# Seven-product blocks in four parts, token factors first, and three weight halves split inside the passages of a two-layer trunk

## The chip, the cores and the metric

The kernel runs on one core of a Trainium2 chip. Its engines work side by side and in the order of their own queues: TensorE (PE) multiplies matrices, and the loading of its stationary operand has a row of its own (PEld); VectorE (DVE) and ScalarE (ACT) work on elements; GpSimd (POOL) and SyncE (SP) issue transfers here. The metric is the device time of one execution in microseconds (us), as the median of several runs. Before the change it is 2310.19 us (three runs, 2307.84 to 2311.49).

## The reference, cut to what matters

256 tokens of width 2048 pass through two layers. Each layer is a mixer (HGRN2 in layer 0, gated linear attention, GLA, in layer 1) and a squared-ReLU MLP of width 8192, each with a norm ahead of it, a norm behind it and a residual add. All is float32.

```python
def rmsnorm(x, w):
    y = xf * lax.rsqrt(jnp.mean(xf * xf, axis=-1, keepdims=True) + NORM_EPS)
    return (y * w.astype(jnp.float32)).astype(x.dtype)

def sqrelu_mlp(h, w_up, w_down):
    u = jax.nn.relu(h @ w_up)
    return (u * u) @ w_down

    for i in range(DEPTH):
        hn = rmsnorm(h, norm_mix_pre[i])
        ...
        h = h + rmsnorm(m, norm_mix_post[i])
        f = sqrelu_mlp(rmsnorm(h, norm_mlp_pre[i]), mlp_w_up[i], mlp_w_down[i])
        h = h + rmsnorm(f, norm_mlp_post[i])
```

## The kernel before, in words

**Two parts per number.** Each float32 matrix operand is split into a rounded part `hi`, made by ACT (L103), and a remainder `lo`, made by DVE (L107); a product is three matmuls (hi·hi, hi·lo, lo·hi) that accumulate. Weights come as chunks of 1 MB in three buffers (`raw`); a chunk is two halves of 128x1024, and each half is split into one of five buffers for `hi` and one of five for `lo` (pool `wsp`). The activations are kept transposed and split (`xhl`).

**Column products.** `gemmT` (L146, L149) makes 128 columns of a result, transposed, from one chunk: 16 matmuls of 512 columns with the `hi` weights, and 16 of 256 with the `lo` weights. `fold` (L155, L156) adds the two parts up. The factor per token (the reciprocal of the norm's root) isn't multiplied into the activations; it is applied to the results: `rrow` (L301, L303) spreads the factors `rs` of the 256 tokens over a tile `rr`, and each folded column product of an MLP is multiplied by it in L537. After it come the square and its split (L539 to L541).

**MLP.** The 8192 features are eight groups `g` of 1024. `up(g)` makes a group's features in eight column products, four for group 0, whose first half comes out of the passage. `combine` (L507 to L512) makes from four of these, by pairs, the sums of activations `as` (`sums_of_a`); they live in memory that the next group's sums reuse. The product of a group with two of the four column blocks of `w_dn` is a 2x2 block product, made with seven block products in place of eight: `seven(g)`. Of the seven, three use plain weights, four use sums of blocks of `w_dn`. These sums (tiles `run` and `Q`, `bs` in the rows) are made by transfers: `begin_run` and `begin_q` load a block on SP's queue (L563, L572), and `add_to` adds another block to it on POOL's queue (L558). Each block product is 12 matmuls of 512 columns into a bank of PSUM, `sa`, `sb` or `sc`, and two weight halves to split; `put` (L578, L580) then adds the bank to the result. The next product into the same bank waits for that. The other two column blocks of `w_dn` are done plainly (`plain`, 48 matmuls and four halves each).

**Order.** A planner orders the instructions on each engine: it takes them in the order of the program's text where they are ready by its own model of time, and pulls later ones ahead where earlier ones aren't. For group 0 and 1 the text is: `up(0)`; the first column product of `up(1)`; all of `seven(0)`; the other seven column products of `up(1)`. From there `down(g)` places the four parts of `seven(g+1)` between the chunks of `plain(g, 2)` and `plain(g, 3)`; `seven` is a generator that yields between its parts.

**Passages.** `transition` is the passage from one sub-layer to the next, three in all: HGRN to MLP 0, MLP 0 to GLA, GLA to MLP 1. It ends the last output block, norms, adds the residual (L340, one instruction per quarter row `n` and token half `t`), transposes `h` on PE (`T_in`, L182), scales and splits it (`T_out`, ACT L193 and DVE L195), and runs the first block of the next sub-layer on weights split ahead (`ahead`, eight halves): `nxt(0, j)` for the tokens of half 0, `nxt(1, j)` for half 1. Inside `manual_schedule` the instructions of PE, ACT, DVE and POOL keep the order of the text; the planner may still put instructions from outside the block between them. The squares of `h` for the token factors (L283, eight of them, `token_rstd`) end the block, and the loop over `nxt(1, j)` stands outside it.

Of the kernel before, what the change touches and what calls it, by code (L numbers as in the profile page):

```python
# [30 lines left out]
def trunk(  # L31
# [77 lines left out]
    def split(raw, into=None):  # L109
# [2 lines left out]
        split_lo(raw, half)  # L112
        return half

    def split_chunk(wap, idx):

        raw = load_chunk(wap, idx)
        return [split(raw[:, hf, :]) for hf in range(2)]

    def mm_half(ps, half, hf, xs, t, nk, kks=(0, 1), cs=slice(0, NB)):  # L120

# [88 lines left out]
    def start(which, w, base):  # L210

        X = Xhl(KT)
        xs = big.tile([P, KT, T], F32, tag="big", name="xs")
        ps = [psmm.tile([P, NB], F32, tag="mm", name=nm("mm")) for _ in range(NT)]
        early = []
        part = small.tile([P, NT, 4], F32, tag="tp", name=nm("tp"))

        def input_quarters(t, qs):  # L220
            for q in qs:
                c = slice(q * NB, (q + 1) * NB)
                nc.sync.dma_start(h[:, t, c], x[t * P:(t + 1) * P, c])
            for q in qs:
                square(part, t, q)

        def next_chunk(c):
            raw = wraw.tile([P, 2, 1024], F32, tag="raw", name=nm("raw"))
            for j in range(2):
                nc.sync.dma_start(raw[:, j, :], w[c].rearrange("p (k n) -> p k n", k=2)[:, j, :])  # L230
            ahead[c] = w, raw
            early.append(gemmT(w, c, X, *((psmm, "mm") if c < 2 else (pssc, "sc"))))

        with tc.manual_schedule(engines=ALL | {mybir.EngineType.SP}):
            for hf in range(KT // 2):
                if hf % 2 == 0:
                    raw = wraw.tile([P, 2, 1024], F32, tag="raw", name=nm("raw"))
                    src = w[base + hf // 2].rearrange("p (k n) -> p k n", k=2)
                for n in range(2 if hf == 0 else 1):

                    m = 2 if hf else 1
                    ks = slice(2 * hf + n, 2 * hf + n + m)
                    cs = slice(n * NB, (n + m) * NB)
                    first = hf == 0 and n == 0
                    nc.sync.dma_start(xs[:, ks, :], xT[:, ks, :])
                    (nc.scalar if first else nc.sync).dma_start(raw[:, hf % 2, cs], src[:, hf % 2, cs])
                    if first:
                        nc.sync.dma_start(prew, npre)
                        A.activation(warm, epsb, AF.Sqrt)
                        for _ in range(4):  # L250
                            idle = pstr.tile([P, T], F32, tag="tr", name=nm("idle"))
                            PE.matmul(idle, bc(epsb, [P, P]), bc(epsb, [P, T]), start=True, stop=True)
                    for k in range(2 * hf + n, 2 * hf + n + m):
                        hi, lo = X.both(k)[:, 0, :], X.both(k)[:, 1, :]
                        g = prew[:, which, k:k + 1]
                        A.activation(hi, xs[:, k, :], AF.Copy, scale=g)
                        V.scalar_tensor_tensor(lo, xs[:, k, :], g, hi.bitcast(F32),
                                               ALU.mult, ALU.subtract)
                    if n == 0:
                        half = (wsp.tile([P, 1024], F32R, tag="hi", name=nm("hi")),  # L260
                                wsp.tile([P, 1024], F32R, tag="lo", name=nm("lo")))
                    A.activation(half[0][:, cs], raw[:, hf % 2, cs], AF.Copy)  # L262
                    V.tensor_tensor(half[1][:, cs], raw[:, hf % 2, cs],  # L263
                                    half[0][:, cs].bitcast(F32), ALU.subtract)
                    if hf == 0:
                        for t in range(NT):
                            mm_half(ps[t], half, hf, X, t, KT, (n,))
                if hf:
                    for t in range(NT):
                        mm_half(ps[t], half, hf, X, t, KT)  # L270
            next_chunk(0)
            next_chunk(1)
            input_quarters(0, (0, 1))
            next_chunk(2)
            input_quarters(0, (2, 3))
            nc.sync.dma_start(ident, ident_in)
            next_chunk(3)
            input_quarters(1, range(4))
            rs = rstd_sum(part)
        return X, rs, ps, early  # L280

    def square(part, t, q):
        A.activation(tok(), h[:, t, q * NB:(q + 1) * NB], AF.Square, accum_out=part[:, t, q:q + 1])  # L283

    def token_rstd():
        part = small.tile([P, NT, 4], F32, tag="tp", name=nm("tp"))
        for t in range(NT):
            for q in range(4):
                square(part, t, q)
        return rstd_sum(part)  # L290

    def rstd_sum(part):
        ss = col(NT)
# [48 lines left out]
    class Next:  # L342

        def __init__(self, w, base, big_first=False):
            self.w, self.base, self.raws, self.parts = w, base, [], []
            self.room = self.rooms(big_first)

        def rooms(self, big_first):  # L350
# [39 lines left out]
    def transition(w, base, nk, xs, post, add, which, ahead):  # L390
# [41 lines left out]
        with tc.manual_schedule(engines=ALL):  # L432
            for j in range(4):
                last(0, j)
            first_use(0)
            last(1, 0)
            last(1, 1)
            post.rstd(0)
            ahead.hi()
            post.residual(0, 0)  # L440
            last(1, 2, (0,))
            T_in(0, 0)
            post.residual(1, 0)
            post.residual(2, 0)
            T_out(0, 0)
            last(1, 2, (1,))
            last(1, 3)
            post.residual(3, 0)
            T_in(0, 1)
            T_out(0, 1)  # L450
            nxt(0, 0)
            first_use(1)
            T_in(0, 2)
            nxt(0, 1)
            post.rstd(1)
            T_out(0, 2)
            post.residual(0, 1)
            T_in(0, 3)
            nxt(0, 2)
            T_out(0, 3)  # L460
            nxt(0, 3)
            ahead.lo()
            post.residual(1, 1)
            nxt(0, 4)
            ahead.split()
            T_in(1, 0)
            T_out(1, 0)
            nxt(0, 5)
            post.residual(2, 1)
            T_in(1, 1)  # L470
            nxt(0, 6)
            T_out(1, 1)
            post.residual(3, 1)
            T_in(1, 2)
            nxt(0, 7)
            T_out(1, 2)
            T_in(1, 3)
            T_out(1, 3)
            rs = token_rstd()
        for j in range(KT // 2):  # L480
            nxt(1, j)
        return X, rs, psn


    def mlp(layer, w_up, w_dn, X, rs, ps0, then=None):
# [27 lines left out]

        sa = {}

        def up(g):

            U = Xhl(GK)
            uT[g] = U
            a = {}  # L520
            js = [j + h for j in range(HK) for h in (0, HK)]
            if g == 0:
                for t in range(NT):
                    s = tok()
                    A.activation(s, ps0[t], AF.Relu, scale=rs[t])
                    A.activation(s, s, AF.Square)
                    ps = transpose4(lambda j: s[:, j * P:(j + 1) * P])
                    put_split(ps, U, 0, t)
                    raw = tok().rearrange("p (a n) -> p a n", a=4)
                    A.copy(raw, ps)  # L530
                    for j in range(HK):
                        a[j, t] = raw[:, j, :]
                rr.append(rrow(rs))
                js = range(HK, GK)
            for j in js:
                u = fold(gemmT(w_up, g * GK + j, X))
                V.scalar_tensor_tensor(u, u, 0.0, rr[0], ALU.max, ALU.mult)  # L537
                hi, lo = U.both(j)[:, 0, :], U.both(j)[:, 1, :]
                A.activation(hi, u, AF.Square)  # L539
                A.activation(u, u, AF.Square)  # L540
                V.tensor_tensor(lo, u, hi.bitcast(F32), ALU.subtract)  # L541
                for t in range(NT):
                    a[j, t] = u[:, t * P:(t + 1) * P]
                if j == js[0]:
                    yield
                    sa[g] = sums_of_a(g)
                if j >= HK:
                    i = j - HK
                    combine(sa[g][i], a[i, 0], a[j, 0], a[i, 1], a[j, 1])

        def block(g, h, n):
# [106 lines left out]
                pass  # L658

        for g in range(NG):  # L660
            it = up(g)
            next(it)
            if g == 0:
                begin_run(0)
                begin_q(0)
            if g == 1:
                rest(seven(0))
            rest(it)
            if g:
                down(g - 1)  # L670
# [349 lines left out]
        post = Post(1)  # L1020
        return outproj(w_gout, O, post, then)

    st = hgrn((2, w_up0, 0))
    st = mlp(0, w_up0, w_dn0, *st, then=(1, w_gin, 16))
    st = gla(*st, then=(3, w_up1, 0))
    mlp(1, w_up1, w_dn1, *st)


# [70 lines left out]
```

## Time and profile before

| | us |
|---|---|
| median of three runs | 2310.19 |
| the profiled execution | 2309.34 |
| its span, first to last instruction | 2307.6 |
| PE busy in the span | 2274.4 (99%) |
| DVE busy | 1720.1 (75%) |
| ACT busy | 1328.5 (58%) |
| POOL busy | 69.4 (3%) |

The times in the rows count from the start of the span, which is 1.7 us shorter than the execution's own time. PE is busy nearly throughout; so what can be won without taking work away is where PE stands, and where its clock (PEclk, 1.00 is the full 2.4 GHz) is lower. PE rows show matmuls that overlap: a matmul of 512 columns is drawn 0.39 us long, and the next starts 0.227 us after it.

### The profile page before, as it was taken

What the parts mean: (1) busy time and instruction counts of PE and PEld (TensorE: products, weight loads), DVE (VectorE), ACT (ScalarE), POOL (GpSimd) and SP (SyncE); (2) the same over time, 40 slices, a digit from 0 to 9 for tenths busy, and PEclk for the clock granted to TensorE, in tenths of its full rate; (3) what the DMA queues carried; (4) which work ended last, traced back from release to release, by engine and by line L of the source; (5) the groups of instructions that cost most, each with busy time, mean ns of one, the idle gap of its engine ahead of it and who ended that gap; (6) DMA issues with size and microseconds to landing.
All of it is one profiled execution on the core that took longest, in us unless ns stands there. A gap on an engine that the chain in (4) does not pass through costs nothing.

```text
span 2307.6 us, 30177 instructions
## 1 busy us (share of the span) xinstructions
PE 2274.4 (99%) x11528; PEld 1931.4 (84%) x11528; DVE 1720.1 (75%) x2575; ACT 1328.5 (58%) x1919; POOL 69.4 (3%) x84
## 2 busy tenths in 40 slices
PE   9999999999999999999999999999999999999998
PEld 7888888877888888888887887887788888888887
DVE  6887877666778778778786767666677877877877
ACT  7555554546555555555566456555655655655654
POOL 0000000000000000000000000000000000000000
PEclk9999999999999999999999999999999999999999
DMA  9544545548897788788764544465788878878875
GB/s 326 173 166 160 177 164 183 184 181 246 244 287 243 247 282 252 245 268 264 247 219 147 200 164 155 162 214 196 231 241 279 257 240 288 249 245 279 253 249 161
DMA packets 82289, 517.53 MB, mean 224 GB/s; under 512 B 9792, under 2 KB 10176, under 8 KB 25696
## 3 DMA queue, kind: packets, MB, share of 16 engines
q1 hardware_dynamic: 70480, 448.23, 53.7%
q0 software_dynamic: 11520, 67.11, 15.4%
q8 instruction: 90, 1.47, 0.2%
q14 instruction: 55, 0.45, 0.1%
q10 hardware_dynamic: 144, 0.26, 0.0%
HBM read 513.47 MB, written 2.10 MB: 223 GB/s over the span
## 4 chain that ended last, share of the span: by engine, by line
PE 94%; DVE 3%; DMA 1%; ACT 1%; issue 1%; SPq 0%; DVEq 0%; ACTq 0%
PE mmT L146 26%; PE mmT L149 14%; PE mm L128 13%; PE mm L127 13%; PE mm L126 13%; PE sa L607 7%; PE sb L607 4%; PE sc L607 2%; PE sc L743 2%; DVE lo L107 1%; DMA bs<-w_dn 1%; PE tr L182 1%; DVE xhl L195 0%; PE sd L778 0%; DMA raw<-w_hin 0%
## 5 line engine op out<-in xcount | busy, mean ns | idle before, releaser
L107 DVE TENSOR_TENSOR lo<-raw,hi 128x1024 fp32r<-128x1024 f32 x744 | 903.2, 1221 | 321.2 <-ACT hi L103 256.6
L103 ACT ACTIVATE hi<-raw 128x1024 fp32r<-128x1024 f32 x744 | 782.1, 1059 | 559.0 <-PE mm L128 248.0
L146 PE MATMUL mmT<-xhl,hi 128*128 128x512 f32 x2704 | 658.4, 392 | 2.8 <-ACT hi L103 2.8
L146 PEld LDWEIGHTS mmT<-xhl,hi 128*128 128x128 f32 x2704 | 497.9, 189 | 101.3 <-ACT hi L103 3.6
L127 PE MATMUL mm<-lo,xhl 128*128 128x512 f32 (+1 forms) x1280 | 498.3, 389 | 1.3 <-DVE lo L263 1.2
L128 PE MATMUL mm<-hi,xhl 128*128 128x512 f32 x1280 | 496.9, 389 | 0.0
L126 PE MATMUL mm<-hi,xhl 128*128 128x512 f32 x1280 | 487.4, 391 | 1.4 <-ACT hi L262 0.8
L149 PEld LDWEIGHTS mmT<-xhl,lo 128*128 128x128 f32 x2704 | 347.7, 191 | 13.6 <-issue 0.5
L149 PE MATMUL mmT<-xhl,lo 128*128 128x256 f32 x2704 | 354.4, 283 | 0.0
L126 PEld LDWEIGHTS mm<-hi,xhl 128*128 128x128 f32 x1280 | 240.6, 188 | 51.7 <-ACT hi L262 2.4
L127 PEld LDWEIGHTS mm<-lo,xhl 128*128 128x128 f32 x1280 | 240.5, 188 | 50.7 <-DVE lo L263 2.7
L128 PEld LDWEIGHTS mm<-hi,xhl 128*128 128x128 f32 x1280 | 240.4, 188 | 49.2 <-issue 0.2
L103 ACT ACTIVATE hi<-bs 128x1024 fp32r<-128x1024 f32 x128 | 135.3, 1059 | 95.2 <-PE mm L128 37.8
L107 DVE TENSOR_TENSOR lo<-bs,hi 128x1024 fp32r<-128x1024 f32 x128 | 153.8, 1221 | 37.4 <-ACT hi L103 33.9
L558 POOL DMA_DIRECT2D bs<-w_dn x80 | 69.2, 865 | 2188.0 <-DMA bs<-w_dn 1186.8
L607 PE MATMUL sb<-hi,as 128*128 128x512 f32 x256 | 91.3, 408 | 9.4 <-ACT as L511 4.5
L541 DVE TENSOR_TENSOR xhl<-half,xhl 128x256 fp32r<-128x256 f32 x120 | 50.6, 422 | 55.9 <-ACT half L540 55.8
L539 ACT ACTIVATE xhl<-half 128x256 fp32r<-128x256 f32 x120 | 49.0, 411 | 65.6 <-DVE half L537 65.5
L607 PE MATMUL sa<-hi,xhl 128*128 128x512 f32 x256 | 84.2, 389 | 0.0
L607 PE MATMUL sa<-hi,as 128*128 128x512 f32 x256 | 84.0, 389 | 0.0
L155 ACT COPY half<-mmT 128x256 f32<-128x256 f32 x169 | 60.8, 360 | 33.3 <-PE mmT L149 33.2
L156 DVE TENSOR_TENSOR half<-mmT,half 128x256 f32<-128x256 f32 x169 | 70.2, 416 | 0.6 <-ACT half L155 0.6
(209 smaller groups left out, 1861.9 us busy)
## 6 DMA issues: line engine op xcount, KB each, us to landing
raw<-w_up SPq DMA_DIRECT2D x128, 1024.0 KB, 7.4
raw<-w_dn SPq DMA_DIRECT2D x112, 1024.0 KB, 4.9
raw<-w_hin SPq DMA_DIRECT2D x56, 1024.0 KB, 4.9
bs<-w_dn POOLq DMA_DIRECT2D x48, 1024.0 KB, 8.7
raw<-w_gin SPq DMA_DIRECT2D x48, 1024.0 KB, 4.9
raw<-w_hout SPq DMA_DIRECT2D x16, 1024.0 KB, 4.9
bs<-w_dn SPq DMA_DIRECT2D x32, 512.0 KB, 8.1
bs<-w_dn SPq DMA_DIRECT2D x16, 1024.0 KB, 9.3
```

Of the source, the lines that this page charges most:

```text
L103: A.activation(hi, raw, AF.Copy)
L107: V.tensor_tensor(half[1], raw, half[0].bitcast(F32), ALU.subtract)
L126: PE.matmul(ps, xh, hi[:, kk, cs], start=(k == 0), stop=False)
L127: PE.matmul(ps, xh, lo[:, kk, cs], start=False, stop=False)
L128: PE.matmul(ps, xl, hi[:, kk, cs], start=False, stop=(k == nk - 1))
L146: PE.matmul(ps, hi, X.both(k), start=(k == 0), stop=False)
L149: PE.matmul(ps[:, 0, :], lo, X.both(k)[:, 0, :], start=False, stop=(k == KT - 1))
L155: A.copy(u, ps[:, 1, :])
L156: V.tensor_tensor(u, ps[:, 0, :], u, ALU.add)
L541: V.tensor_tensor(lo, u, hi.bitcast(F32), ALU.subtract)
L558: nc.gpsimd.dma_start(raw, b, accum_op=ALU.add)
L607: PE.matmul(bank[b], l, r[:, kk, :], start=first and j + kk + i == 0, stop=j + kk + i == 4, skip_group_check=not first)
```

## The change

Four things are done.

- `up` yields after each column product in place of after the first alone, and takes `held`: the number of the column product after which the memory for the group's sums is taken and from which `combine` runs; pairs that are ready sooner wait in a list. Group 1 is run with `held=4`, and its column products stand between the four parts of `seven(0)`: after its second, third, fourth and fifth column product comes one part.
- `rrow(rs)` is the first thing in `up(0)`; it was behind the work on the passage's block.
- In `transition` the four squares of token half 0 move ahead to behind `ahead.lo()`; at the end of the fixed order three weight halves of the next stage are split (`split_early`, with their chunks' loads), then come the squares of half 1, then all `nxt(1, j)`, now inside the block, and the factors.
- `early` keeps such split halves until `split_chunk` asks for them; a list and a flag in `start` are renamed for it.

```diff
+    early = {}
+
+    def split_early(wap, idx, count):
+        raw = load_chunk(wap, idx)
+        early[wap.tensor.name, idx] = raw, [split(raw[:, hf, :]) for hf in range(count)]
+
     def split_chunk(wap, idx):
-        raw = load_chunk(wap, idx)
-        return [split(raw[:, hf, :]) for hf in range(2)]
+        raw, halves = early.pop((wap.tensor.name, idx), (None, []))
+        if raw is None:
+            raw = load_chunk(wap, idx)
+        return halves + [split(raw[:, hf, :]) for hf in range(len(halves), 2)]
...
             T_out(0, 3)
             nxt(0, 3)
             ahead.lo()
+            part = small.tile([P, NT, 4], F32, tag="tp", name=nm("tp"))
+            for q in range(4):
+                square(part, 0, q)
             post.residual(1, 1)
...
             T_out(1, 3)
-            rs = token_rstd()
-        for j in range(KT // 2):
-            nxt(1, j)
+            for chunk in ahead.then:
+                split_early(*chunk)
+            for q in range(4):
+                square(part, 1, q)
+            for j in range(KT // 2):
+                nxt(1, j)
+            rs = rstd_sum(part)
...
-        def up(g):
+        def up(g, held=0):
...
             if g == 0:
+                rr.append(rrow(rs))
                 for t in range(NT):
...
-                rr.append(rrow(rs))
                 js = range(HK, GK)
-            for j in js:
+            pairs = []
+            for n, j in enumerate(js):
                 u = fold(gemmT(w_up, g * GK + j, X))
...
-                if j == js[0]:
-                    yield
+                if j >= HK:
+                    pairs.append((j - HK, j))
+                yield
+                if n == held:
                     sa[g] = sums_of_a(g)
-                if j >= HK:
-                    i = j - HK
+                while pairs and n >= held:
+                    i, j = pairs.pop(0)
                     combine(sa[g][i], a[i, 0], a[j, 0], a[i, 1], a[j, 1])
...
-            it = up(g)
+            it = up(g, 4 if g == 1 else 0)
             next(it)
...
             if g == 1:
-                rest(seven(0))
+                next(it)
+                for _ in seven(0):
+                    next(it)
             rest(it)
...
-    st = hgrn((2, w_up0, 0))
-    st = mlp(0, w_up0, w_dn0, *st, then=(1, w_gin, 16))
-    st = gla(*st, then=(3, w_up1, 0))
+    st = hgrn((2, w_up0, 0, ((w_up0, 4, 2), (w_up0, 5, 1))))
+    st = mlp(0, w_up0, w_dn0, *st, then=(1, w_gin, 16, ((w_gr, 0, 2), (w_gin, 20, 1))))
+    st = gla(*st, then=(3, w_up1, 0, ((w_up1, 4, 2), (w_up1, 5, 1))))
```

## Rows read from the trace of the kernel before

**Rows 1.** The page's first part: busy time, share of the span, instructions.

```profile
PE 2274.4 (99%) x11528; PEld 1931.4 (84%) x11528; DVE 1720.1 (75%) x2575; ACT 1328.5 (58%) x1919; POOL 69.4 (3%) x84
```

**Rows 2.** Stretches: length, busy time of each engine, clock, DMA share, GB/s.

```profile
507.53:510.22 2.69, 0.62 (x3) 0.19 (x1) 2.69 (x5) 0.07 (x1) 0.00 (x0) 1.00 0.85 311
510.22:513.98 3.76, 3.76 (x10) 2.95 (x11) 3.08 (x9) 0.00 (x0) 0.00 (x0) 0.55 0.81 322
...
1211.70:1214.40 2.70, 0.42 (x2) 0.00 (x0) 2.70 (x5) 0.10 (x1) 0.00 (x0) 1.00 0.92 322
...
1610.40:1612.80 2.40, 0.36 (x2) 0.00 (x0) 2.40 (x4) 0.00 (x0) 0.00 (x0) 1.00 0.76 314
1612.80:1616.50 3.70, 3.70 (x9) 2.96 (x10) 3.08 (x9) 0.00 (x0) 0.00 (x0) 0.54 0.82 330
```

**Rows 3.** Timeline of the first passage: start, length, engine, line; then idle before.

```profile
501.59 3.94 ACT L103 ACTIVATE hi<-raw 128x1024 fp32r<-128x1024 f32 x4
...
505.28 4.63 DVE L107 TENSOR_TENSOR lo<-raw,hi 128x1024 fp32r<-128x1024 f32 x4
...
509.82 1.12 DVE L195 SCALAR_TENSOR_TENSOR xhl<-tr,prew,xhl 128x128 fp32r<-128x128 f32 x4
510.22 0.67 PE L128 MATMUL mm<-sqk,xhl 128*128 128x512 f32 x1 [2.07 <-DVE xhl L195]
510.86 0.74 DVE L340 SCALAR_TENSOR_TENSOR h<-tok,col,h 128x512 f32<-128x512 f32 x1
...
519.95 0.65 ACT L283 ACTIVATE tok<-h 128x512 f32<-128x512 f32 x1
```

**Rows 4.** Timeline: the tile of factors in MLP 0.

```profile
534.25 0.41 DVE L156 TENSOR_TENSOR half<-mmT,half 128x256 f32<-128x256 f32 x1
...
540.78 0.61 PE L301 MATMUL psr<-ident,col 128*128 128x128 f32 x4
...
545.25 0.36 ACT L303 COPY rr<-psr 128x256 f32<-128x256 f32 x1
...
547.13 0.75 DVE L537 SCALAR_TENSOR_TENSOR half<-half,rr 128x256 f32<-128x256 f32 x2
```

**Rows 5.** Stretches of both MLPs, columns as in rows 2.

```profile
553.70:566.06 12.36, 8.85 (x36) 5.87 (x34) 12.36 (x25) 9.93 (x15) 0.40 (x1) 0.96 0.90 247
566.06:575.05 8.99, 6.88 (x15) 4.60 (x15) 6.32 (x9) 2.11 (x2) 0.86 (x1) 0.50 0.98 245
575.05:591.48 16.43, 15.28 (x74) 12.64 (x73) 11.49 (x14) 8.85 (x10) 2.59 (x3) 0.99 0.95 265
...
712.00:753.00 41.00, 41.00 (x182) 33.96 (x181) 33.35 (x39) 24.89 (x26) 2.59 (x3) 1.00 0.93 277
...
1664.00:1674.60 10.60, 5.73 (x14) 3.86 (x14) 7.93 (x12) 4.35 (x6) 0.86 (x1) 0.68 0.88 236
1674.60:1691.90 17.30, 15.65 (x77) 12.91 (x76) 12.33 (x14) 8.89 (x10) 2.59 (x3) 1.00 0.94 265
```

**Rows 6.** The chain that ended last: start, length, engine, tile, line, count.

```profile
570.19 5.35 PE sb L607 x12
...
670.48 3.65 PE mmT L146 x16
676.04 3.65 PE mmT L146 x16
...
716.95 2.72 PE sa L607 x12
...
1670.51 4.79 PE sb L607 x12
```

**Rows 7.** Line L558, the adds on POOL's queue, from 500 to 680 us.

```profile
DMA to landing us min/median/max: 5.8/9.8/15.6
```

**Rows 8.** DVE's groups from 553.70 to 591.50: count, busy, mean ns of one.

```profile
L512 DVE TENSOR_TENSOR as<-tok,as 128x512 fp32r<-128x512 f32 x4 | 2.7, 678 | 0.0
...
L510 DVE TENSOR_TENSOR tok<-tok,half 128x128 f32<-128x128 f32 x4 | 1.1, 279 | 0.0
```

More of the change, by code (lines that the diff above doesn't have):

```diff
@@ L216, in start @@
         ps = [psmm.tile([P, NB], F32, tag="mm", name=nm("mm")) for _ in range(NT)]
-        early = []
+        first = []
         part = small.tile([P, NT, 4], F32, tag="tp", name=nm("tp"))
@@ L231, in next_chunk @@
             ahead[c] = w, raw
-            early.append(gemmT(w, c, X, *((psmm, "mm") if c < 2 else (pssc, "sc"))))
+            first.append(gemmT(w, c, X, *((psmm, "mm") if c < 2 else (pssc, "sc"))))
         with tc.manual_schedule(engines=ALL | {mybir.EngineType.SP}):
@@ L243, in start @@
                     cs = slice(n * NB, (n + m) * NB)
-                    first = hf == 0 and n == 0
+                    lead = hf == 0 and n == 0
                     nc.sync.dma_start(xs[:, ks, :], xT[:, ks, :])
-                    (nc.scalar if first else nc.sync).dma_start(raw[:, hf % 2, cs], src[:, hf % 2, cs])
-                    if first:
+                    (nc.scalar if lead else nc.sync).dma_start(raw[:, hf % 2, cs], src[:, hf % 2, cs])
+                    if lead:
                         nc.sync.dma_start(prew, npre)
@@ L279, in start @@
             rs = rstd_sum(part)
-        return X, rs, ps, early
+        return X, rs, ps, first
     def square(part, t, q):
         A.activation(tok(), h[:, t, q * NB:(q + 1) * NB], AF.Square, accum_out=part[:, t, q:q + 1])
[L285 to L290, printed above, removed]
     def rstd_sum(part):
@@ L342, in trunk, with __init__ @@
     class Next:
-        def __init__(self, w, base, big_first=False):
-            self.w, self.base, self.raws, self.parts = w, base, [], []
+        def __init__(self, w, base, then, big_first=False):
+            self.w, self.base, self.then, self.raws, self.parts = w, base, then, [], []
             self.room = self.rooms(big_first)
```

## Prediction

> **What bounds the kernel now.** I read the busy times first: PE is busy for 2274.4 of 2307.6 us [rows 1]. The change removes no matmul and adds none, so it can only win the 33.2 us in which PE stands and the time that a halved clock costs. Next I cut the span into stretches and looked for those in which PE isn't full. Besides the start and the end there are two kinds, and the change touches both.
>
> The first kind is the three passages. PE stands 2.07 us in the first (2.69 long, 0.62 busy), 2.28 in the second and 2.04 in the third; behind the first and third the clock is at about half, 1.2 GHz, for 3.76 and 3.70 us, a loss of 3.76 x 0.45 = 1.69 and 3.70 x 0.46 = 1.70 [rows 2]. Behind the second it stays up, though that pause was the longest. Sum: 9.8 us.
>
> The second kind is `seven(0)` in either MLP. In MLP 0 PE stands 3.51 + 2.11 + 1.15 = 6.8 us between 553.70 and 591.48, in MLP 1 4.87 + 1.65 = 6.5 us [rows 5]. The clock is at half in the middle: twelve matmuls took 5.35 us and 4.79 us where twelve take 2.72 [rows 6], 2.63 and 2.07 lost, and with three and one slow ones before them, at 0.2 each, 3.2 and 2.3. Sum: 10.0 and 8.8, together 18.8 us.
>
> All in all 28.6 us are there to be won. Why PE stands is in the DVE column: it is busy for 12.36 of 12.36 us when the trouble begins. The same seven block products in later groups, placed between plain chunks, leave PE busy for 41.00 of 41.00 us with DVE at 33.35 [rows 5].
>
> **The change part by part. Passages.** In the first passage DVE makes four `lo` in one run of 4.63 us from 505.28 on; one belongs to the passage, three are weights of the next stage that the planner had pulled in. The `lo` of `T_out(1,0)` starts only at 509.82, and PE waits for it until 510.22 [rows 3]. The change puts these three splits behind `T_out(1,3)`: 3 x 1.16 = 3.5 us earlier, `T_out(1,0)` starts at 506.3 and ends at 507.4. Can other splits slip in instead? They need a buffer of the five in `wsp`; the last two halves of `ahead` and the three early ones hold all five until `nxt(1,6)`. So no.
>
> ACT loses three `hi` there (three quarters of 3.94, 3.0 us) and gets four squares (4 x 0.65 = 2.6 us) [rows 3], so what follows on it is no later. But a new order is set: all `nxt(1,j)`, which PE took up while it waited, now stand behind `T_in(1,2)` and `T_in(1,3)`. `T_in(1,2)` needs `residual(2,1)`, 0.74 us on DVE behind `T_out(1,0)`: about 508.3. PE has nothing from 507.53 on, as no new weights are split yet: a pause of 0.9 us with semaphores. It can be between nothing (if `T_in(1,1)` and `nxt(0,6)` move too) and the present 2.07; I take 0.9, in all three, as the rows of the other two repeat the pattern. A pause of 0.42 ahead of the second one, for `residual(1,1)`, stays. After 0.9 us I expect no fall of the clock, as 2.28 us passed without one. From there on nothing is late: `T_out(1,3)` ends on DVE about 513.5, `nxt(1,6)`, its first user, comes at 519. The three splits (3.5 us of DVE, 3.0 of ACT) and four squares lie beside 10.9 us of `nxt(1,j)`, at no cost; their loads go out on SP in the old order, and the three `hi` ran at 501.59 without a wait, so their data lay there. If that cover were gone, the wait would be the lateness of the load. Passages: 9.8 - 3 x 0.9 = 7.1 us won.
>
> **Factors first.** The squares ended late (the first began at 519.95), `rrow`'s matmuls ran at 540.78, `rr` was there at 545.25, and the first column product, folded at 534.25, waited for its factor until 547.13 [rows 4]. So the squares, splits and combinations of group 0 pile up from 547 on and fall on DVE together with the splits of `seven(0)`. After: four squares at ACT's about 515 to 518, the factors about 519, `rrow` about 522 when `nxt(1,7)` is through. PE's work is the same (0.61 us); DVE's is spread over 30 us. This carries part of the 18.8 us, and I don't price it apart.
>
> **Four parts.** From the first block product to the last, PE now has 7 x 2.72 + 3 x 5.56 = 35.7 us of work [rows 6]: a column product is 676.04 - 670.48. What does DVE need beside it? The stretch of a later group has 22 `lo`, eleven puts and strays in 33.35 us. Take out eight `lo` (8 x 1.16) and four puts (4 x 0.68), put in three column products (each two `lo` and three steps of 0.38, 3.5) and the two combinations held back (each 4 x 0.28 + 0.68 = 1.8 [rows 8]): 33.35 - 9.3 - 2.7 + 10.4 + 3.6 = 35.4. That is an upper end, as the stretch has some 2.4 us of strays. 33 to 35.4 of 35.7: full, not over, and five split halves lie ready when it begins. Banks: `a` is now left alone for a column product between its uses, where 570.19 to 572 had it and `b` back to back. `held`: five of six `half` tiles stay taken until the fifth column product; the sixth serves the next, and two combinations (3.6 us) free four under its 5.56 us of PE. Cost nothing, or one such chain if DVE is behind.
>
> What is late next? `begin_q(1)` and `begin_run(1)` now go out behind three or four more weight loads on SP and have less time: from the load of `run` to its use PE has 2.72 + 3 x 5.56 + 5.45 = 24.9 us, less 2.2 for splitting it, 22.7. In the trace the load came at 579.69 and the add behind it 9 us later; adds land after 9.8 us in the median, 15.6 at most [rows 7]. So 18.8 to 24.6: 0 to 1.9 us late. ACT would wait in that split, with the next plain halves queued behind it, and PE behind both. Bounds for what stays in one MLP: 0 (the later groups) to 2; I take 1. MLPs: 18.8 - 2 = 16.8 us won.
>
> **Sum.** 7.1 + 16.8 = 23.9 us from the profiled execution's 2309.34: 2285.4. The median of the runs lies 0.85 above that execution: 2286.
>
> **The rivals.** *A part stays.* DVE at up to 99% and a late `run(1)` hold PE for 3 to 6 us in each MLP, with a half clock once: 8 to 13 us won less, 2291 to 2301. For: DVE's sum, ACT's waits. Against: the early factors empty DVE's queue before.
>
> *The planner undoes it.* Its model saw no stall where the trace has them; if it pulls the column products ahead of the block products as before, only the passages win: about 2303. Or the fixed order makes pauses of 2 us with a slow clock again and nothing moves: 2306 to 2314.
>
> *Slower: the transfers become the bound.* The mixed stage wants three plain blocks, six for `run` and `Q` and three column chunks, twelve of 1.05 MB in 35.7 us, 353 GB/s if all must land in it. Between 566.06 and 575.05 the transfer engines were 0.98 taken and moved 245 GB/s [rows 5], as adds move fewer bytes. At that rate 12.6 MB take 51 us: 15 us of pause in each MLP, 31 together, more than the 25.9 that the rest wins: some 5 us slower, 2315. It turns at 12.9 us of pause in each, about 260 GB/s. Against it: the later groups want thirteen blocks in 41 us and got 277 GB/s in the stretch, and PE never stood [rows 5]; what they lacked had been loaded before or came after, and the last four blocks of the mixed stage aren't wanted in it either. The Trainium skill's page "DMA: Bandwidth & Descriptors", section "Issuing engines are not separate DMA queues", says that transfers issued by different engines run on the same 16 DMA engines and interleave; by it the adds on POOL's queue would take time from SP's weight loads, which is this rival. No row here separates the two queues' shares within the stage.
>
> **How the numbers follow.** Forecast (2281 to 2291) 0.66; a part stays 0.20; only the passages 0.06; no change 0.05; slower 0.03. Measurements of this kernel tell about 0.2%, 4.6 us, from no change. Faster by more: 0.66 + 0.20 + 0.06 = 0.92; within: 0.05; slower: 0.03. The lower end is all 28.6 us won, 2281.6, less a little for the spread of runs: 2280; the upper end takes in most of "a part stays": 2299.
>
> **What would show it.** Right: in the first passage DVE's `lo` run is split, one then three behind the last L195, and PE's pause there is about 0.9 us at clock 1.00; L301 runs near 522; the stretch of `seven(0)` has PE full, sa, sb and sc rows with L146 between them, and clock 1.00. Wrong: ACT L103 on `bs` waiting for DMA near the end of `up(1)` with a PE pause after it (the late `run`), DVE without a gap while PE waits for `lo` or `as`, or a PE wait of 2 us for L340 in the passages.

## The result and the profile after

The changed kernel takes 2281.05 us in the median of four runs (2280.48 to 2281.44), the kernel before, beside it on the same chip, 2309.02 (2307.77 to 2311.49). The ratio is 0.9878, with a 95% interval of 0.9866 to 0.9890: 28.0 us less. The forecast was 2286, and the result lies in its forecast case, 2281 to 2291, at the lower edge.

The first line of the page of after, as in [rows 1]: busy time, share of the span, instructions. The span is now 2279.4 us.

```profile
PE 2263.6 (99%) x11528; PEld 1925.7 (84%) x11528; DVE 1719.5 (75%) x2575; ACT 1330.1 (58%) x1919; POOL 69.6 (3%) x84
```

PE's instructions are the same in number. Span less busy time was 33.2 us and is 15.8, so 17.4 us of standing went. The other 10.8 us came out of the busy time (2274.4 to 2263.6): a matmul at half clock is drawn longer, and so is the first one behind a pause.

The first passage of after, ACT's, DVE's and PE's timelines, answering [rows 3]. The squares (L283 before) are L292 now, L195 is L204, L340 is L343 and L182 is L191.

```profile
501.31 0.68 ACT L292 ACTIVATE tok<-h 128x512 f32<-128x512 f32 x1
...
505.01 1.22 DVE L107 TENSOR_TENSOR lo<-raw,hi 128x1024 fp32r<-128x1024 f32 x1
506.14 1.12 DVE L204 SCALAR_TENSOR_TENSOR xhl<-tr,prew,xhl 128x128 fp32r<-128x128 f32 x4
507.18 0.74 DVE L343 SCALAR_TENSOR_TENSOR h<-tok,col,h 128x512 f32<-128x512 f32 x1
507.98 0.66 PE L191 MATMUL tr<-ident,h 128*128 128x128 f32 x4 [0.54 <-DVE h L343]
...
512.72 3.49 DVE L107 TENSOR_TENSOR lo<-raw,hi 128x1024 fp32r<-128x1024 f32 x3
...
1195.62 0.66 PE L191 MATMUL tr<-ident,h 128*128 128x128 f32 x4 [0.44 <-DVE h L343]
1198.45 0.66 PE L191 MATMUL tr<-ident,h 128*128 128x128 f32 x4 [0.80 <-DVE h L343]
1595.28 0.66 PE L191 MATMUL tr<-ident,h 128*128 128x128 f32 x4 [0.54 <-DVE h L343]
```

DVE's run of four `lo` has become one and three. `T_out(1, 0)` begins at 506.14, where it began at 509.82, and PE waits 0.54 us in place of 2.07, now for the residual (`h`). The pause is where the working had put it. The last three lines are the only waits of this kind that are left in the second and third passage.

The factors of MLP 0, answering [rows 4] (L156 is L165, L301 is L304, L303 is L306, L537 is L548), and the stretch of `seven(0)` in both MLPs, answering [rows 5]; columns of the last two lines as there.

```profile
522.37 0.61 PE L304 MATMUL psr<-ident,col 128*128 128x128 f32 x4
...
523.01 0.38 ACT L306 COPY rr<-psr 128x256 f32<-128x256 f32 x1 [0.52 <-PE psr L304]
...
529.27 0.42 DVE L165 TENSOR_TENSOR half<-mmT,half 128x256 f32<-128x256 f32 x1
529.73 0.43 DVE L548 SCALAR_TENSOR_TENSOR half<-half,rr 128x256 f32<-128x256 f32 x1
...
555.97:591.50 35.53, 35.53 (x181) 30.34 (x180) 31.31 (x39) 23.51 (x31) 2.60 (x3) 1.00 0.91 289
1643.28:1679.00 35.72, 35.72 (x182) 30.53 (x181) 32.35 (x42) 24.29 (x33) 2.60 (x3) 1.00 0.97 301
```

The factor `rr` is there before the first fold; it came 11.00 us behind it. PE is full through both stretches, at full clock. The chain of work in them, [rows 6], now goes to and fro between block products and column products:

```profile
556.13 2.07 PE sb L620 x9
558.20 1.59 PE sa L620 x7
559.78 0.91 PE mmT L155 x4
...
567.14 2.75 PE sc L620 x12
...
580.86 2.75 PE sa L620 x12
583.61 3.63 PE mmT L155 x16
```

What is late next is the tail of the stage, as the working had feared. Waits of ACT, and PE's only waits behind them that the timeline shows:

```profile
599.49 1.06 ACT L103 ACTIVATE hi<-raw 128x1024 fp32r<-128x1024 f32 x1 [4.68 <-DMA raw<-w_dn]
607.60 1.06 ACT L103 ACTIVATE hi<-bs 128x1024 fp32r<-128x1024 f32 x1 [4.79 <-DMA bs<-w_dn]
...
631.76 0.50 PE L620 MATMUL sa<-lo,as 128*128 128x512 f32 x1 [0.29 <-DVE lo L107]
...
1718.25 0.50 PE L620 MATMUL sa<-lo,as 128*128 128x512 f32 x1 [0.32 <-DVE lo L107]
```

ACT stands 4.79 us for the late `run(1)`, but PE still has split halves in front of it and loses little. The chain that ended last runs through that addition (594.77, 12.74 us to its landing) to PE's pause of 0.29 us at 631.76.

### The profile page after: what moved, and what is told of

It reads as the page before. It is cut to its first block, busy times and chain, and to the rows that moved or that the text cites. A ratio compares the mean times of both kernels' runs of the same rounds, so it can differ in the third digit from the quotient of the medians.

```text
span 2279.4 us, 30175 instructions
## 1 busy us (share of the span) xinstructions
PE 2263.6 (99%) x11528; PEld 1925.7 (84%) x11528; DVE 1719.5 (75%) x2575; ACT 1330.1 (58%) x1919; POOL 69.6 (3%) x84
## 3 DMA queue, kind: packets, MB, share of 16 engines
q1 hardware_dynamic: 70480, 448.23, 54.2%
q0 software_dynamic: 11520, 67.11, 15.5%
## 4 chain that ended last, share of the span: by engine, by line
PE 93%; DVE 3%; DMA 2%; ACT 1%; issue 0%; SPq 0%; DVEq 0%; ACTq 0%
PE mmT L155 26%; PE mmT L158 14%; PE mm L137 12%; PE mm L136 12%; PE mm L135 12%; PE sa L620 7%; PE sb L620 3%; PE sc L620 2%; PE sc L758 2%; DVE lo L107 1%; DMA bs<-w_dn 1%; DMA raw<-w_dn 1%; PE tr L191 1%; DVE xhl L204 1%; PE sd L793 0%
## 5 line engine op out<-in xcount | busy, mean ns | idle before, releaser
L165 DVE TENSOR_TENSOR half<-mmT,half 128x256 f32<-128x256 f32 x169 | 70.5, 418 | 0.6 <-ACT half L164 0.6
```

The lines of the kernel that those rows point to most:

```text
L165: V.tensor_tensor(u, ps[:, 0, :], u, ALU.add)
```

## The experiments

**One part, or two, of the three.** The change was cut into the four parts of `seven(0)`, the passages (squares moved, three splits early, `nxt(1, j)` in the fixed order) and the factors (`rrow` first), and all combinations were run. First each alone.

```diff
 # only the passages: the new transition and split_early; up, rrow and the loop over g as before
```

> The kernel before with the change in the passages alone; the text order of seven(0) and the place of rrow are as before. By the prediction's terms the three passages win 9.8 us of pauses and slow clock less what stays (0.54, 0.82 and 0.54 us in the trace of the changed kernel), some 8 us: about 2301 us, and the stretch of seven(0) still stands 6 to 7 us with a halved clock in each MLP. Rival (the gain is only handed on): an earlier end of the passage makes the wait in seven(0) longer by as much, and the time stays within 3 us of 2309.

```diff
 # only the parts
-                rest(seven(0))
+                next(it)
+                for _ in seven(0):
+                    next(it)
```

> The kernel before with seven(0) of both MLPs in four parts between the column products, held=4, and nothing else. If the bunching of the splits of seven(0) is the main cause, 14 to 18 of the 18.8 us go: 2291 to 2295 us. Rival (late factors are the cause): rr still comes near 545 and the combinations of group 0 still pile up, PE pauses for as in the first part, and no more than 6 us go: 2303 us or more.

```diff
 # only the factors
             if g == 0:
+                rr.append(rrow(rs))
...
-                rr.append(rrow(rs))
```

> The kernel before with rrow moved to the head of up(0) alone. The combinations of group 0 spread out, but the seven block products still stand back to back, for which DVE needs as much time as PE, and with two uses of one bank in a row: I expect half of the 18.8 us, about 2300 us, with the pause for as gone and the pauses for put and for the column product's weights left. Rival one (the factors are the whole cause): 2291 us or less. Rival two (they cost nothing, as the planner had PE busy until 553.7): 2307 us or more.

```diff
 # all but the parts: the changed kernel with
-            it = up(g, 4 if g == 1 else 0)
+            it = up(g)
...
-                next(it)
-                for _ in seven(0):
-                    next(it)
+                rest(seven(0))
```

> The changed kernel with seven(0) in one piece again; factors first and the passages stay. If the parts of the gain add up, this is the changed kernel plus what factors alone leave of the stalls in seven(0), 2281 + 9 = 2290 us. If the early factors make the four parts needless, within 2 us of 2281. If without the four parts the earlier work brings nothing in the MLPs, 2300 us.

Then the two pairs that have the parts:

```diff
 # all but the passages: the changed kernel with transition's end as before
-            for chunk in ahead.then:
-                split_early(*chunk)
...
 # all but the factors: the changed kernel with rrow behind the passage's block
-                rr.append(rrow(rs))
```

> The change without its part in the passages: the four parts and the early factors stay; the squares stand at the end of the fixed order again, no weight half is split early, and nxt(1, j) is outside the order. Theory (the parts of the change add up only once seven(0) stands in four parts): the three passages pause for about 2 us each again, two with a half clock behind them, 9.8 us in the rows of before against 1.9 us of pauses that the changed kernel still has there, so some 8 us slower than the changed kernel: 2289, within 2286 to 2291. Rival (the passages bring nothing, as they did when made alone): 2280 to 2283.

> The change without the early factors: rrow stands behind the work on the passage's block again; the four parts and the passages stay. Theory (factors first takes DVE's squares, splits and combinations out of the mixed stage, and with the four parts that is worth what the kernel with the parts alone lost there: 1.7 us of PE in either MLP and the clock behind it): 3 to 8 us slower than the changed kernel, 2284 to 2289, I take 2286. Rival (factors first brings nothing or costs 4 us, as it did when made alone): 2277 to 2282.

Measured, with the ratio to the kernel before from runs on the same chip:

| parts | passages | factors | median us | ratio, 95% interval |
|---|---|---|---|---|
| – | yes | – | 2307.78 | 0.9994 (0.9985 to 1.0004) |
| – | – | yes | 2313.49 | 1.0016 (1.0006 to 1.0025) |
| – | yes | yes | 2306.89 | 0.9994 (0.9984 to 1.0003) |
| yes | – | – | 2296.67 | 0.9942 (0.9927 to 0.9957) |
| yes | – | yes | 2289.52 | 0.9913 (0.9898 to 0.9928) |
| yes | yes | – | 2281.17 | 0.9878 (0.9863 to 0.9892) |
| yes | yes | yes | 2281.05 | 0.9878 (0.9866 to 0.9890) |

Of the six expectations only that for `no_passages` held in its number. `only_parts` came nearest to its theory but missed its range by 1.7 us: 12.2 of the 18.8 us went, where 14 to 18 were put. In `only_passages`, `only_factors` and `no_factors` it was the rival that came, and `no_parts` came out above all three numbers that had been named for it. Where `no_passages` expected half clocks behind two of its pauses, its trace shows the pauses (2.04, 2.30 and 2.04 us) and a clock of 1.00 behind all three.

Without the four parts nothing brings the kernel below the time before: the passages alone are worth nothing, and the factors alone cost 4.6 us (2313.49 against 2308.90 on the same chip), which the passages make good. With the parts, the passages are worth 2296.67 - 2281.17 = 15.5 us without the early `rrow` and 2289.52 - 2281.05 = 8.5 with it; the factors are worth 7.2 us without the passages and nothing with them. (By the ratios, which allow for the chips, it is 14.8, 8.1 and 6.7 us.) So the terms of the sum don't add. No run separates `held` from the placing of the parts. Two questions follow: where does the passages' gain go when `seven(0)` is in one piece, and why are the factors worth 7 us only without the passages?

**Where the gain goes.** The passages' gain is there in the trace of `only_passages`: the last `nxt` runs at 521.36, at 527.86 before. Of these 6.5 us, 3.4 are 15 matmuls of column products (at 0.227 us) that PE had taken up ahead of it before; some 3 us are won. They are gone 50 us later. (The profiled execution took 2312.30 us, 4.5 above the median of its ten runs.) The stretches that hold `seven(0)`, of `only_passages`, columns as in [rows 2]:

```profile
550.00:595.00 45.00, 35.34 (x140) 27.62 (x139) 31.27 (x45) 21.93 (x29) 3.46 (x4) 0.85 0.89 238
1645.00:1695.00 50.00, 40.87 (x174) 32.29 (x174) 35.29 (x54) 26.15 (x37) 4.33 (x5) 0.86 0.82 228
```

The same stretches of before have PE busy for 38.23 and 43.48 us at clock 0.89 and 0.93. One wait has grown in both MLPs; in MLP 0 it reads:

```profile
574.93 2.00 ACT L103 ACTIVATE hi<-bs 128x1024 fp32r<-128x1024 f32 x2 [6.77 <-DMA bs<-w_dn]
...
577.93 3.78 PE L155 MATMUL mmT<-xhl,hi 128*128 128x512 f32 x8 [5.50 <-ACT hi L103]
```

In MLP 1 it is 5.12 us for ACT and 4.41 for PE, which goes on at 1679.88; before it went on at 1679.69, although all three passages have been shortened by then. The trace of `no_parts` shows what PE stands for; POOL's add, ACT's split and PE's matmul, with the idle time before each:

```profile
563.42 0.86 POOL L571 DMA_DIRECT2D bs<-w_dn  x1 [13.78 <-DVE lo L107]
...
572.16 2.00 ACT L103 ACTIVATE hi<-bs 128x1024 fp32r<-128x1024 f32 x2 [4.36 <-DMA bs<-w_dn]
...
575.16 1.22 PE L155 MATMUL mmT<-xhl,hi 128*128 128x512 f32 x2 [3.67 <-ACT hi L103]
```

The tile `run` is split three times in `seven(0)`: for the first product, after an addition for the fifth, and after a second addition for the last. That second addition can't go out before DVE's `lo` of the fifth product is made, and ACT begins the split 8.7 us after it went out. In one piece only one other block product (2.72 us, [rows 6]) stands between. ACT waits for it in its queue, the `hi` of the next column product stands behind that, and PE behind both. Before the change ACT's wait there was 2.00 us and PE's 1.15 (1.65 in MLP 1), as PE's waits for `as` and `tok` and its half clock came while the transfer was under way; the fewer of them, the longer ACT waits. (In `only_passages` the addition also took longer: it went out at 563.78, 11.2 us ahead of the split, where it was 8.3 before.) That was read; to test it, the second addition was left out.

```diff
 # no_parts, with
-            add_to(run[1], block(g, 1, 0))
+            if g:
+                add_to(run[1], block(g, 1, 0))
```

> The kernel with everything but the four parts (2306.9 in one piece), and of the first group's sums of blocks the second addition into the tile run is left out, in either MLP; so the last of the seven products uses a sum that lacks one block. Theory (in one piece the last product waits for that addition, which can start only when run's second half has been split and lands some 9 us later; ACT stands in that split for 4.4 us and the next column product behind it for 3.7 us, in either MLP, and that is where the gain of the passages went): ACT's wait on the transfer and PE's wait for ACT's hi behind it go, 7.5 us and part of the slow clock, 2295 to 2300. Rival (DVE's splits and combinations at the start of the stage are the bound, as the prediction had it, and the transfer only fills that time): 2304 to 2308.

Measured: 2297.63 us (0.9948, 0.9934 to 0.9963), 9.3 less than `no_parts`, as the theory had it. Less traffic isn't the reason in MLP 0: between 553 and 592 us of `no_parts` ACT waited for no other transfer. PE's waits in `no_parts_no_add` (us in total, times, longest):

```profile
PE sb L620 <- DVE as L522: 3.2, 2, 1.6
PE sb L620 <- ACT as L521: 2.6, 3, 1.3
PE tr L191 <- DVE h L343: 2.5, 4, 0.8
PE sb L620 <- DVE tok L591: 2.5, 2, 1.2
PE mmT L155 <- ACT hi L103: 2.3, 2, 1.1
```

The last line was 7.5 us in two in `no_parts`, so 5.2 us of standing went; with them the clock rose, from 0.91 to 0.97 between 540 and 600 us and from 0.89 to 0.97 between 1640 and 1700. What stays of that line, 1.15 us in either MLP, is in MLP 0 all that PE stood there before the change: the transfer cost PE nothing there as long as other waits covered it. The waits for `as` and `tok`, DVE's and ACT's work to which the prediction had charged the stage, are still there. So a transfer into a tile that is reused was the bound behind the bound. With the four parts two column products more (5.56 us each, [rows 6]) stand between the second addition and its use.

**Why the factors count only once.** In `no_factors` `rr` is there at 533.93 us, though `rrow` stands late in the text, and in `no_passages` at 529.64, though the squares are late; with the parts alone it is 543.57, and in the kernel before 545.25. The early squares and the early `rrow` seem to be two ways to one end. So both were taken away, with the early splits and the order of `nxt(1, j)` kept.

```diff
 # the changed kernel with rrow as before, and
-            for q in range(4):
-                square(part, 0, q)
             post.residual(1, 1)
...
-            for q in range(4):
-                square(part, 1, q)
             for j in range(KT // 2):
                 nxt(1, j)
+            for t in range(NT):
+                for q in range(4):
+                    square(part, t, q)
             rs = rstd_sum(part)
```

> The change with the factors late in both senses: all eight squares stand behind the nxt(1, j) at the end of the fixed order, and rrow behind the work on the passage's block; the three early splits, the order of nxt(1, j) and the four parts stay. Theory (in the MLP it is the time at which rr is there that counts, and either the early squares or the early rrow brings it from 544 to 534 or earlier, so that taking away one of them cost nothing): with both gone the MLPs lose what the kernel with the parts alone lost there, 7 us: 2288, within 2285 to 2291, and the first L548 begins behind 540. Rival (rr's time doesn't matter; the early splits or the order of nxt(1, j) carry the MLPs' gain): 2280 to 2283.

Measured: 2285.62 us (0.9895, 0.9878 to 0.9911), 4.6 more than the changed kernel; the first L547 (the product with `rr`) begins at 541.42. That is within the theory's bounds, near the lower one, and less than the 7 us expected. By the ratios it is 3.9 us, and their intervals overlap; the runs themselves don't (2284.52 to 2287.66 against 2280.48 to 2281.44). Stretches of `late_factors`:

```profile
600.00:650.00 50.00, 48.74 (x225) 38.95 (x224) 39.55 (x53) 28.33 (x38) 3.46 (x4) 1.00 0.82 260
1650.00:1700.00 50.00, 49.33 (x262) 42.39 (x261) 40.57 (x59) 28.14 (x38) 3.46 (x4) 1.00 0.96 302
1700.00:1750.00 50.00, 47.94 (x211) 39.08 (x210) 41.79 (x53) 29.89 (x36) 4.33 (x5) 0.97 0.84 271
```

and of after:

```profile
600.00:650.00 50.00, 49.56 (x230) 40.32 (x229) 41.12 (x55) 29.52 (x38) 3.46 (x4) 1.00 0.84 271
1650.00:1700.00 50.00, 50.00 (x267) 43.28 (x266) 40.19 (x62) 30.78 (x43) 3.46 (x4) 1.00 0.94 299
1700.00:1750.00 50.00, 49.68 (x234) 41.27 (x234) 40.62 (x50) 27.74 (x33) 4.33 (x5) 1.00 0.92 286
```

PE stands 3.99 us against 0.76, behind the mixed stage and in its tail: late factors make the chain of splits and additions late, and `run(1)` with it. In MLP 0 its addition goes out at 596.36 in place of 594.77, and ACT waits 6.66 us for it in place of 4.79. The clock falls once, in the last of these stretches.

**The early splits.**

```diff
 # the changed kernel with
-            for chunk in ahead.then:
-                split_early(*chunk)
```

> The change without the three weight halves split early; nxt(1, j) stand in the fixed order and the squares are early as in the change. Theory (three weight halves that the planner pulls into the passage ahead of T_out(1, 0) are what made PE wait, and the early split places them): the planner has the buffers to pull them in ahead of T_out(1, 0) again, pauses of about 2 us with half clocks in the passages, 2286 to 2291, I take 2288. Rival (the fixed place of nxt(1, j) and of the squares alone settles the passages): the pauses stay at 0.5 to 0.8 us, 2280 to 2284.

Measured: 2297.16 us (0.9947, 0.9932 to 0.9962), 16.1 more than the changed kernel and worse than the theory's upper end. The planner pulled three splits in again:

```profile
505.29 4.62 DVE L107 TENSOR_TENSOR lo<-raw,hi 128x1024 fp32r<-128x1024 f32 x4
509.83 1.12 DVE L204 SCALAR_TENSOR_TENSOR xhl<-tr,prew,xhl 128x128 fp32r<-128x128 f32 x4
...
511.67 0.88 PE L191 MATMUL tr<-ident,h 128*128 128x128 f32 x4 [3.94 <-DVE h L343]
```

That is the run of [rows 3], and now `nxt(1, j)` can't fill the pause, as the fixed order holds them behind `T_in(1, 2)`: 3.94 us in place of 2.07. The other two passages have 4.21 and 3.94 us, and behind all three pauses the clock is 0.72 to 0.73 for some 6 us. The two halves of the passage's edit need each other: the fixed place of `nxt(1, j)` without the splits costs more than the passages as they were (`no_passages`, 2289.52).

**The pauses that are left.** Three steps of the fixed order were moved.

```diff
-            ahead.lo()
...
             post.residual(1, 1)
+            ahead.lo()
...
+            nxt(0, 7)
             T_in(1, 2)
-            nxt(0, 7)
             T_out(1, 2)
+            nxt(1, 0)
             T_in(1, 3)
...
-            for j in range(KT // 2):
+            for j in range(1, KT // 2):
```

> The changed kernel with three steps of the passage's fixed order moved: nxt(0, 7) ahead of T_in(1, 2), nxt(1, 0) between T_out(1, 2) and T_in(1, 3), and ahead.lo() behind residual(1, 1). Theory (the pauses left in the passages, 0.54, 0.44 and 0.80, and 0.54 us, are waits of T_in for the residual on DVE with work for PE standing behind it in the order): 2.3 us of pauses and some 0.1 us each for the first slow matmul go: 2278.4, within 2277.5 to 2279.5, and no wait of T_in for DVE is left. Rival (what is moved makes the next step late, and the pause only changes its place): 2280.5 to 2283.

Measured: 2280.94 us (0.9875, 0.9858 to 0.9891), no different from the changed kernel. All four waits of `T_in` for the residual went from the passages. In their place MLP 1 has one that was not there:

```profile
1621.55 0.66 PE L191 MATMUL tr<-ident,tok 128*128 128x128 f32 x4 [1.31 <-ACT tok L538]
```

and in MLP 0 PE stands 0.71 us between 600 and 650 in place of 0.44. 2.3 us won, 1.6 given back, the rest below what the runs tell apart: the rival.

**Transfers.** The rival that would have made the kernel slower was tried by adding transfers to the changed kernel.

```diff
 # extra_load: eight transfers in either MLP, between the parts
+                nc.sync.dma_start(out[...], w_dn[...][:, :1024])
 # extra_store: twelve of 256 KB, that read features of the second group
+                nc.sync.dma_start(out[...], uT[1].both(...).bitcast(F32))
```

> The changed kernel with eight transfers more in the mixed stage of either MLP, 4.2 MB in all, from w_dn to rows of the result that are written anew later; they go out on SP's queue between the parts and nothing waits for their data. They test the rival in which the transfers bound the stage. At the 245 to 350 GB/s of the stage's rows they take 12 to 17 us of the transfer engines. Mine (the stage has room for transfers: the engines were 0.69 to 0.77 taken in some stretches of 8 us between 540 and 612): a part of them shows, 2 to 6 us of pause in either MLP, 2285 to 2293. Rival (the transfers are as good as the bound already): nearly all of it shows, 10 us or more in either MLP, 2301 to 2315.

> The changed kernel with twelve transfers more in either MLP, 256 KB each, 3.1 MB in all, from the features of the second group to rows of the result that are written anew later. They can't start before the column products of the mixed stage whose features they read; the extra transfers of the run before depended on nothing, and the planner put them at the start of the program. At the 245 to 350 GB/s of the stage's rows they take 9 to 13 us of the transfer engines. Mine (the stage has room for transfers): 1 to 4 us of pause in either MLP, 2283 to 2289, with longer waits of ACT for raw and bs. Rival (the transfers are as good as the bound): 8 us or more in either MLP, 2297 to 2307.

The first missed its aim. It took 2290.29 us (0.9916, 0.9901 to 0.9931), inside my range, but for another reason:

```profile
L671 SPq DMA_DIRECT2D out<-w_dn x16: 511/532/1381, 19.5 to 68.1; - x16
```

All sixteen went out between 19.5 and 68.1 us, at the start of the program, and held up the first weights: of the first two stretches of 50 us PE was busy for 45.60 and 46.22 us, where after has 46.95 and 50.00. It says nothing on the MLPs. In the second they went out in MLP 0 at 558, 562, 573 and 596 us, three at a time. It took 2282.19 us (0.9878, 0.9861 to 0.9894), no different from the changed kernel. Stretches of `extra_store`, columns as in [rows 2]:

```profile
560.00:570.00 10.00, 10.00 (x53) 8.59 (x52) 8.65 (x12) 6.79 (x10) 0.00 (x0) 1.00 1.01 374
570.00:580.00 10.00, 10.00 (x52) 8.52 (x51) 8.98 (x11) 6.52 (x8) 0.86 (x1) 1.00 1.02 303
580.00:590.00 10.00, 10.00 (x55) 8.67 (x55) 7.67 (x10) 6.22 (x9) 1.71 (x2) 1.00 1.03 393
```

Where after moved 293, 254 and 340 GB/s, 374, 303 and 393 went through, and PE never stood. The rival is refuted, and my pause of 1 to 4 us in either MLP was too high.

## Why the prediction was right

**The bound.** It held: PE's standing and slow matmuls gave 17.4 + 10.8 = 28.2 us of the span, and no work was taken away. That is nearly the 28.6 us counted as avoidable, though 2.6 us of the counted pauses stayed: the slow matmuls had been counted too low (below).

**The passages.** The mechanism, the place and the wait that remains were right; the pause was put at 0.9 us and is 0.54, 0.80 and 0.54. No half clock followed. That the clock would hold was argued from the one pause of 2.28 us that had passed without a fall, and such pauses go either way: of nine of 2.04 to 2.32 us in the traces of before, `only_parts` and `no_passages`, four have a half clock behind them. `no_splits` shows that the three splits had to be placed by hand; that they would then leave no room for others held.

**Factors first.** The times were right: the squares run from 514.36 on and L304 at 522.37, for 515 and "about 522". "This carries part of the 18.8 us, and I don't price it apart" was wrong as far as `rrow` goes: it carries nothing beside the early squares. The same paragraph counts both as one, and together they carry 4.6 us (`late_factors`).

**Four parts.** PE full in the stage, by a sum of DVE's work of 33 to 35.4 us: DVE has 31.31 and 32.35, so the sum was high by 2 us or more, above all because the two combinations (3.6 us) that it put into the stretch come behind it. The late `run(1)` came, and ACT's wait of 4.79 us is more than the 0 to 1.9 forecast. The transfers were as put: from the load at 584.63 to the landing at 607.51 they took 22.9 us, within 18.8 to 24.6. But the working gave ACT 22.7 us, by PE's work; ACT runs ahead of PE and came to the split 18.2 us after the load. The same lead spared PE, which stood 0.44 us in MLP 0 and 0.32 in MLP 1 where 1 us each was put for "PE behind both".

**The sum.** 23.9 us were forecast from the profiled execution's 2309.34; its counterpart of after took 2281.16, so 28.2 came. The mis-sized terms: pauses of the passages 2.7 us put, 1.88 measured (0.8); pauses of the MLPs 2.0 put, 0.76 measured (1.2); and slow matmuls, counted as 1.69 + 1.70 + 3.2 + 2.3 = 8.9 where the busy time fell by 10.8 (1.9). That is 3.9 of the 4.3.

**What it didn't see.** The sum took passages, factors and parts as independent terms. The table shows that they aren't: the passages alone were worth 0 and not 7.1, and the rival "only the passages: about 2303" would have come out at 2308. The trace of before had the sign of it: ACT's split of `bs` waited for a transfer in the stage of the trouble, and I charged that stage to DVE, since DVE was busy for 12.36 of 12.36 us when it began [rows 5]. The forecast of the whole was right because the parts, which remove that bound, were in it. That was luck as far as the passages go: nothing in the working asked whether their 7.1 us need the parts.

**Transfers as the bound.** The slower rival read a ceiling in 245 GB/s at 0.98 taken [rows 5]. `extra_store` moved 393 GB/s in the same stage. The working said that no row separates the two queues; the page of before does for the whole execution (packets, MB, share of the 16 engines' span), SP's loads first and then the additions:

```profile
q1 hardware_dynamic: 70480, 448.23, 53.7%
q0 software_dynamic: 11520, 67.11, 15.4%
```

Per MB the additions took 1.9 times as much of the engines, so a high share at a low rate can come of additions and need not be a limit. The Trainium skill's page "DMA: Bandwidth & Descriptors", section "Issuing engines are not separate DMA queues", has transfers of different issuers interleave on the same engines. MLP 0 agrees: with the stores on SP's queue the median landing of POOL's five adds of 1 MB went from 8.8 to 10.5 us and that of `w_up` loads on SP from 6.6 to 8.8. In MLP 1 the loads went from 6.8 to 8.4, but the adds stayed (8.7 and 8.6), so there the runs don't show it between the two queues. PE waited for none of it.

## What to carry to other kernels

Gains ahead of a stage count only if the stage can take them up: before adding terms, look in each stage behind for a wait on something that doesn't get faster with the rest, a transfer into a reused tile above all: what stalled ahead of it had covered it, and without these stalls its wait grows. An engine that is busy at the start of a pause need not be what ends it; follow the queue of the engine that made the late operand. When a planner orders the work, an edit that fixes the place of the filler has to fix the place of what the filler waited for too.

## What the runs showed of the hardware

A busy share of the transfer engines near 1.0 did not tell what they could still take: 0.98 went with 245 GB/s while additions ran, and 1.03 with 393 GB/s when plain stores were added. Over the whole execution before, additions took 15.4% of the engines for 67.11 MB and SP's transfers 53.7% for 448.23 MB.

In the kernel after, pauses of PE of 0.29 to 0.80 us left the granted clock at 1.00 in every stretch of 25 us around them; the first matmul of 512 columns behind those of 0.29 and 0.32 us is drawn 0.50 us long against 0.39. Pauses of 2.04 to 2.32 us in the passages went both ways: the clock fell behind the first and third before the change, behind the second and third in `only_parts`, and behind none in `no_passages`.
